# A two-layer backbone on one core: the last part of a layer split into latent and context tokens, each half's norm put beside products of the other half

## The chip, the cores and the metric

One core of one Trainium2 chip. The time is the device time of one execution in microseconds, median of the runs. TensorE (PE in the profile) does the matrix products, with its weight loads shown apart (PEld); VectorE is DVE, ScalarE is ACT, GpSimd is POOL, and SyncE (SP) issues most of the transfers.

## What is computed

Two layers over a stream of 256 context and 512 latent tokens of 1024 channels. The reference, cut:

```python
for l in range(DEPTH):                       # 2 layers
    ctx_out = l < DEPTH - 1                  # the last layer gives only latent tokens
    mod_l = split(silu(c) @ w_mod[l] + b_mod[l], 6); mod_c = split(silu(c_ctx) @ w_mod[l] + b_mod[l], 6)
    hc = modulate(xc, norm_mix_pre[l], mod_c[0], mod_c[1])
    hl = modulate(xl, norm_mix_pre[l], mod_l[0], mod_l[1])
    oc, ol = token_mixer(hc, hl, ..., w_in[l], rw, cv, at, w_branch[l], w_out[l], ctx_out)
    xl = xl + mod_l[2] * rms_norm(ol, norm_mix_post[l])
    hl = modulate(xl, norm_mlp_pre[l], mod_l[3], mod_l[4])
    xl = xl + mod_l[5] * rms_norm(sq_relu_mlp(hl, w_ff1[l], w_ff2[l]), norm_mlp_post[l])
    if ctx_out:                              # the same three lines for xc, with mod_c
        ...
return xl
def modulate(x, g, shift, scale): return rms_norm(x, g) * (1 + scale) + shift
# token_mixer: z = h @ w_in; three branches (RWKV-7, convolution, attention), each @ w_branch,
# summed with sigmoid gates (columns of z), then @ w_out
```

## The kernel before

All activations lie transposed: 128 channels on the partitions, eight such tiles k, tokens along the free axis, context in columns 0 to 255 and latent tokens in 256 to 767. `TOK` is 768. Layer 0 works on all 768 tokens, which a product takes as two pieces of 384; layer 1's last part works on the 512 latent ones (`T` = 512).

A float32 product is made of three products of a narrower format: activation and weight are split in a high and a low part (hh and hl or fh and fl, oh and ol; wh and wl), and high by high, low by high and high by low are summed. A tile of 128 output channels is 8 k x 3 products per piece. A weight tile comes as two halves of 256 KB (`weight_half`): a transfer into raw on SP's queue (two buffers), wh on ScalarE and wl on VectorE (three buffers). `gemm` makes a tile at once; `job` puts a tile in a list, and `fill(n)` takes n of its k steps from it, so that tiles can be woven between other work. The order in which each engine gets its instructions is settled by a scheduler when the program is built, which starts from the order of the code.

The last part of a layer goes: three branch projections (`branch` in `merge_phase`, with gates gt, sum in acc), acc halved and split into oh and ol, eight w_out tiles, the norm of their result (`ss_slow` sums squares, `rstd` makes 1/root as a column and TensorE spreads it into R), `post_norm` (scale acc, add to the residual X, square it again), a second `rstd`, `norm_h` (modulated and split into hh and hl). Then in `mlp_phase` four quarters q, each of eight ff1 tiles (squared relu, split into fh and fl) and eight ff2 tiles added into acc; and after the last quarter the same chain of norms again, now with the next layer's first modulation. Its hh and hl feed the next layer's projection, `rwkv_phase`. In that, tiles of z go to memory through `spill`; rows 28 to 31 of the list are four gate tiles, and `todo` and `SCHED` say how many tiles are made at which of eight head pairs.

The modulation vectors come from w_mod in steps of 1 MB (`mod_steps`, tile wmod, two buffers, loaded by ScalarE's queue): eight a group, 16 of them for layer 0 between the branch and w_out tiles, 24 for layer 1, one behind each ff1 tile of the first three quarters.

Of the kernel before, what the change touches and what calls it, by code (L numbers as in the profile page):

```python
# [8 lines left out]
F32 = mybir.dt.float32  # L9
# [9 lines left out]
D = 1024  # L19
# [29 lines left out]
         dict(open=1.2, first=0.4, mid=0.4, end=0.4, solve=34, early=5, tap0=0.8, tap1=0.8, merge=1.4, sums=0, grams=0, rest=9, ln=9, pad=1, last=0.85, tap2=1.1)]  # L49
# [27 lines left out]
class Kern:  # L77
# [48 lines left out]
    def dv(s, ap, T):  # L126

        return ap.rearrange("p (a b) -> p a b", b=384) if T == TOK else ap[:, CTX:TOK]

# [203 lines left out]

    def norm_h(s, sp, X, R, T, gs, sh, hh, hl):

        nc = s.nc
        o = TOK - T
        for k in range(KT):
            t = sp.tile([128, TOK], F32, tag="nt", name="nt", bufs=2)
            for b, t0, t1 in s.pieces(T, CTX):  # L340
                v = 1 if t0 < CTX else 0
                sl = slice(t0, t1)
                nc.vector.scalar_tensor_tensor(out=t[:, sl], in0=X[:, k, sl], scalar=gs[:, k, v:v + 1], in1=R[:, b, :t1 - t0], op0=ALU.mult, op1=ALU.mult)
                if k % 2:
                    nc.scalar.activation(out=t[:, sl], in_=t[:, sl], func=AF.Identity, bias=sh[:, k, v:v + 1])
                else:
                    nc.scalar.activation(out=hh[:, k, sl], in_=t[:, sl], func=AF.Identity, bias=sh[:, k, v:v + 1])  # L347
                    nc.vector.scalar_tensor_tensor(out=hl[:, k, sl], in0=t[:, sl], scalar=sh[:, k, v:v + 1], in1=hh[:, k, sl].bitcast(F32), op0=ALU.add, op1=ALU.subtract)
            if k % 2:
                s.split(hh[:, k, o:], hl[:, k, o:], t[:, o:], True)  # L350

    def post_norm(s, sp, A, X, R, T, gm, each):

        nc = s.nc
        o = TOK - T
        for k in range(KT):
            for b, t0, t1 in s.pieces(T, CTX):
                v = 1 if t0 < CTX else 0
                nc.vector.scalar_tensor_tensor(out=A[:, k, t0:t1], in0=A[:, k, t0:t1], scalar=gm[:, k, v:v + 1], in1=R[:, b, :t1 - t0], op0=ALU.mult, op1=ALU.mult)
            eng = nc.gpsimd if k % 2 else nc.vector  # L360
            eng.tensor_tensor(out=X[:, k, o:], in0=X[:, k, o:], in1=A[:, k, o:], op=ALU.add)
            each(k)
# [29 lines left out]
    def job(s, src, mh, ml, T, done, pre=None):  # L392

        s.halves += [(src, h) for h in range(2)]
        s.jobs += [(k, mh, ml, T, done, pre) for k in range(KT)]

    def fill(s, n=1):
        nc = s.nc
        for _ in range(min(n, len(s.jobs))):
            k, mh, ml, T, done, pre = s.jobs.pop(0)  # L400
# [8 lines left out]
            for w, m, f in ((wh, mh, 0), (wh, ml, 1), (wl, mh, 2)):  # L409
                a = m(k)  # L410
                for b, t0, t1 in s.pieces(T):
                    s.last_mm = nc.tensor.matmul(s.jps[:, b, :t1 - t0], lhsT=w[:, k % 4, :], rhs=a[:, t0:t1], start=k == 0 and f == 0, stop=k == KT - 1 and f == 2)  # L412
# [662 lines left out]
    def spill(s, l, r, T):  # L1075

        c0, t, f = s.spills[r]
        T = TOK if t else T
        s.in_job(l, c0, T, lambda ps: s.spill_done(r, T, f, ps))

    def spill_done(s, r, T, tanh, ps):
        nc = s.nc
        ft = s.stage()
        if tanh:
            nc.scalar.activation(out=s.dv(ft, T), in_=s.pv(ps, T), func=AF.Tanh, scale=0.5)
        else:
            nc.scalar.activation(out=s.dv(ft, T), in_=s.pv(ps, T), func=AF.Copy)
        nc.scalar.dma_start(s.z[128 * r:128 * r + 128, TOK - T:], ft[:, TOK - T:])


    def run(s):
# [13 lines left out]
        s.z = s.dp.tile([128 * len(s.spills), TOK], F32, name="z")  # L1105
        s.kp = lambda d: d.rearrange("(k p) t -> p k t", p=128)
# [15 lines left out]
        for l in range(DEPTH):  # L1122
# [5 lines left out]
            s.h_open()  # L1128
            s.mlp_phase(l, PP, T, acc, actx)
# [9 lines left out]
    def rwkv_phase(s, l, P, T):  # L1139
# [3 lines left out]
        with ExitStack() as rc:  # L1143
# [21 lines left out]
            todo = list(range(20)) + list(range(28, 36)) + list(range(20, 28))  # L1165

# [82 lines left out]
    def merge_phase(s, l, PP, T, acc):  # L1249
# [4 lines left out]
        with ExitStack() as mc:  # L1254
# [67 lines left out]
            drive(ln, 3)  # L1322
            s.fill(len(s.jobs))
            branch(1, *operand(lambda k: cvx[k]))
            for j in range(KT):
                s.fill(8)
                if steps:
                    steps.pop(0)()
            for k in range(KT):
                nc.vector.tensor_scalar(out=acc[:, k, o:], in0=acc[:, k, o:], scalar1=0.5, scalar2=None, op0=ALU.mult)  # L1330
            hs, ls = operand(lambda k: acc[:, k])
            s.ss = s.ps2()

            def done(j, ps):
                nc.scalar.activation(out=s.dv(acc[:, j], T), in_=s.pv(ps, T), func=AF.Copy)
                s.ss_slow(lp, s.ss, acc[:, j], j, T)
            for j in range(KT):
                s.job(i['w_out'][l, :, 128 * j:128 * j + 128], lambda k: hs[k], lambda k: ls[k], T, lambda ps, j=j: done(j, ps))
            for j in range(KT):
                s.fill(8)  # L1340
                if steps:
                    steps.pop(0)()
            if l == 0:
                s.mod_post(P)
            s.R = s.rstd(lp, s.ss, T, 1.0 / D, 0, CTX)

    def mlp_phase(s, l, PP, T, acc, actx):
# [5 lines left out]
        if not last:  # L1353
            PP.append(s.load_params(l + 1))
        X = actx.enter_context(tc.tile_pool(name="x", bufs=1)).tile([128, KT, TOK], F32, name="X")
        for k in range(KT):
            nc.sync.dma_start(X[:, k, o:], s.xT_d[128 * k:128 * k + 128, o:])
        with tc.tile_pool(name="n1", bufs=1) as sp:
            ss = s.ps2()
            s.post_norm(sp, acc, X, s.R, T, P['gm'][0], lambda k: s.ss_add(sp, ss, X[:, k], k, T))  # L1360
            R = s.rstd(sp, ss, T, 1.0 / D, 0, CTX)
            s.norm_h(sp, X, R, T, P['gs'][1], P['sh'][1], s.hh, s.hl)
        with tc.tile_pool(name="mlp", bufs=1) as sp:
            steps = [f for g in range(3) for f in s.mod_steps(l + 1, PP[l + 1], sp, g, 2)] if not last else []
            for q in range(4):
                fhs, fls = [], []
                for j in range(KT):
                    c = q * D + 128 * j
                    ps = s.gemm(i['w_ff1'][l, :, c:c + 128], lambda k: s.hh[:, k], lambda k: s.hl[:, k], T)
                    f = sp.tile([128, TOK], F32, tag="f", name="f", bufs=2)  # L1370
                    nc.scalar.activation(out=s.dv(f, T), in_=s.pv(ps, T), func=AF.Relu)
                    nc.vector.tensor_tensor(out=f[:, o:], in0=f[:, o:], in1=f[:, o:], op=ALU.mult)
                    fh = sp.tile([128, TOK], F32R, tag="fh", name="fh", bufs=8)
                    fl = sp.tile([128, TOK], F32R, tag="fl", name="fl", bufs=8)
                    s.split(fh[:, o:], fl[:, o:], f[:, o:])
                    fhs.append(fh)
                    fls.append(fl)
                    if steps:
                        steps.pop(0)()
                if q == 3:  # L1380
                    ss = s.ps2()
                for j in range(KT):
                    ps = s.gemm(i['w_ff2'][l, q * D:(q + 1) * D, 128 * j:128 * j + 128], lambda k: fhs[k], lambda k: fls[k], T)
                    if q == 0:
                        nc.scalar.activation(out=s.dv(acc[:, j], T), in_=s.pv(ps, T), func=AF.Copy)
                    else:
                        nc.vector.tensor_tensor(out=s.dv(acc[:, j], T), in0=s.dv(acc[:, j], T), in1=s.pv(ps, T), op=ALU.add)
                    if q == 3:
                        s.ss_slow(sp, ss, acc[:, j], j, T)
            if not last:  # L1390
                s.mod_pre(PP[l + 1])
                s.mod_post(PP[l + 1])
            s.R = s.rstd(sp, ss, T, 1.0 / D, 0, CTX, tag="sq")
        with tc.tile_pool(name="n2", bufs=1) as sp:
            if last:
                s.post_norm(sp, acc, X, s.R, T, P['gm'][1], lambda k: None)
                s.store_x(sp, X)
            else:
                ss = s.ps2()
                s.post_norm(sp, acc, X, s.R, T, P['gm'][1], lambda k: s.ss_add(sp, ss, X[:, k], k, T))  # L1400
                R = s.rstd(sp, ss, T, 1.0 / D, 0, CTX)
                N = PP[l + 1]
                s.norm_h(sp, X, R, T, N['gs'][0], N['sh'][0], s.hh, s.hl)
                nc.sync.dma_start(s.kp(s.xT_d), X)
        actx.close()
# [13 lines left out]
    def store_x(s, sp, X):  # L1419
        nc = s.nc  # L1420
        for t in range(4):
# [37 lines left out]
```

## Time and profile before

| | |
|---|---|
| median of 3 runs | 4373.27 us (4359.16 to 4374.07) |
| the profiled execution | 4372.14 us, span of its instructions 4370.4 us |
| mean granted TensorE clock | 0.963 |
| TensorE busy | 4141.8 us, 95% |
| VectorE, ScalarE, GpSimd busy | 2723.4 us, 1834.4 us, 287.1 us |

Busy time is an average over stages; the table says only that TensorE is nearly full. Times in the rows are from the start of the span. An idle time is put down to what ended last before the engine went on.

### The profile page before, as it was taken

To read this page: it belongs to the slowest core of one execution; us is meant where nothing else is said; L and a number is where in the kernel's file an instruction comes from. 1 tells how busy PE (TensorE), PEld (TensorE's weight loads), DVE (VectorE), ACT (ScalarE), POOL (GpSimd) and SP (SyncE) were. 2 spreads that over 40 slices of the span, in tenths; PEclk is the share of its full clock that TensorE was granted. 3 is DMA by queue.
4 is the path that set the end of the run, shared out by engine and by line. 5 is a ranking of instruction groups with operands and counts; after the bars stand their busy time and mean duration, and the time that the engine had idled before them with its cause. 6 is when DMAs were issued, how large, how long until landed. Compare 5 with 4: busy or idle time off the path is not lost.

```text
span 4370.4 us, 77114 instructions
## 1 busy us (share of the span) xinstructions
PE 4141.8 (95%) x31232; PEld 3410.5 (78%) x31232; DVE 2723.4 (62%) x5238; ACT 1834.4 (42%) x3586; POOL 287.1 (7%) x349
## 2 busy tenths in 40 slices
PE   6999999999998989899999899999999989898998
PEld 4888888888886679689999677887777765575886
DVE  3788888888855554332323577888888855554344
ACT  3444445444534442332223445555545534433332
POOL 0000000000001022200000100000000000121001
PEclk9999999999999999899999889999999979998998
DMA  4212211112134234343322221112221232242332
GB/s 165 78 47 63 64 53 60 51 55 63 59 100 163 69 120 160 110 152 126 102 86 63 72 70 51 58 59 60 66 62 57 73 119 74 65 140 61 97 94 80
DMA packets 443595, 367.73 MB, mean 84 GB/s; under 512 B 19662, under 2 KB 391528, under 8 KB 437096
## 3 DMA queue, kind: packets, MB, share of 16 engines
q1 hardware_dynamic: 422504, 283.10, 21.6%
q10 hardware_dynamic: 20736, 79.70, 5.0%
q8 instruction: 247, 4.05, 0.4%
q14 instruction: 108, 0.88, 0.1%
HBM read 301.38 MB, written 53.48 MB: 81 GB/s over the span
## 4 chain that ended last, share of the span: by engine, by line
PE 80%; DVE 9%; ACT 5%; issue 2%; DMA 2%; POOL 2%; SPq 0%; ACTq 0%; DVEq 0%; POOLq 0%
PE mm L412 31%; PE mm L389 20%; PE g L815 3%; PE g L633 2%; PE g L939 2%; PE sp L960 2%; PE g L928 2%; PE S L612 2%; PE sp L964 1%; PE yp L978 1%; PE yp L976 1%; PE g L850 1%; PE g L1044 1%; PE g L824 1%; PE g L234 1%
## 5 line engine op out<-in xcount | busy, mean ns | idle before, releaser
L328 ACT ACTIVATE wh<-raw 128x512 fp32r<-128x512 f32 x700 | 441.4, 631 | 1249.8 <-PE mm L389 565.5
L332 DVE TENSOR_TENSOR wl<-raw,wh 128x512 fp32r<-128x512 f32 x700 | 502.0, 718 | 697.6 <-ACT wh L328 685.3
L412 PE MATMUL mm<-hh,wh 128*128 128x384 f32 (+1 forms) x2072 | 647.5, 371 | 15.3 <-ACT hh L328 4.8
L412 PE MATMUL mm<-hl,wh 128*128 128x384 f32 (+1 forms) x2072 | 637.9, 367 | 6.1 <-POOL hl L330 6.1
L412 PE MATMUL mm<-hh,wl 128*128 128x384 f32 (+1 forms) x2072 | 634.8, 365 | 0.0
L471 DVE SCALAR_TENSOR_TENSOR cv<-u,dw,cv 128x783 f32<-128x783 f32 (+1 forms) x480 | 426.7, 889 | 2.8
L412 PEld LDWEIGHTS mm<-hh,wh 128*128 128x128 f32 x2072 | 377.6, 192 | 55.1 <-ACT hh L328 7.3
L412 PEld LDWEIGHTS mm<-hl,wh 128*128 128x128 f32 x2072 | 382.6, 192 | 38.0 <-POOL hl L330 8.8
L412 PEld LDWEIGHTS mm<-hh,wl 128*128 128x128 f32 x2072 | 383.0, 192 | 30.5 <-issue 3.2
L412 PE MATMUL mm<-oh,wh 128*128 128x384 f32 (+1 forms) x768 | 252.9, 384 | 9.5 <-DVE acc L1285 6.0
L412 PE MATMUL mm<-ol,wh 128*128 128x384 f32 (+1 forms) x768 | 239.9, 365 | 10.2 <-POOL ol L330 10.2
L389 PE MATMUL mm<-hh,wh 128*128 128x384 f32 (+1 forms) x768 | 239.5, 367 | 5.3 <-ACT hh L347 3.6
L389 PE MATMUL mm<-hl,wh 128*128 128x384 f32 (+1 forms) x768 | 238.3, 365 | 5.1 <-POOL hl L330 4.6
L412 PE MATMUL mm<-oh,wl 128*128 128x384 f32 (+1 forms) x768 | 238.8, 364 | 0.0
L389 PE MATMUL mm<-hh,wl 128*128 128x384 f32 (+1 forms) x768 | 235.8, 362 | 0.0
L389 PE MATMUL mm<-fh,wh 128*128 128x384 f32 (+1 forms) x768 | 229.9, 353 | 0.0
L389 PE MATMUL mm<-fh,wl 128*128 128x384 f32 (+1 forms) x768 | 229.9, 353 | 0.0
L389 PE MATMUL mm<-fl,wh 128*128 128x384 f32 (+1 forms) x768 | 229.5, 352 | 0.0
L815 PEld LDWEIGHTS g<-KR,BK 64*128 64x128 f32 x1536 | 157.3, 204 | 43.0 <-issue 33.7
L815 PE MATMUL g<-KR,BK 64*128 64x128 f32 (+1 forms) x1536 | 178.3, 306 | 5.2 <-DVE KR L808 3.1
L412 PEld LDWEIGHTS mm<-oh,wh 128*128 128x128 f32 x768 | 139.6, 189 | 51.2 <-ACT wh L328 13.6
L966 ACT ACTIVATE S<-sp,lam 128x64 f32<-128x64 f32 x352 | 92.9, 310 | 206.3 <-PE sp L964 199.4
(297 smaller groups left out, 7239.0 us busy)
## 6 DMA issues: line engine op xcount, KB each, us to landing
raw<-in_w_in_dram SPq DMA_DIRECT2D x316, 256.0 KB
raw<-in_w_ff_dram SPq DMA_DIRECT2D x256, 256.0 KB
wmod<-in_w_mod_dram ACTq DMA_DIRECT2D x48, 1024.0 KB
raw<-in_w_branch_dram SPq DMA_DIRECT2D x96, 256.0 KB
z<-f ACTq DMA_DIRECT2D x40, 384.0 KB
gt<-z SPq DMA_DIRECT2D x24, 384.0 KB
raw<-in_w_out_dram SPq DMA_DIRECT2D x32, 256.0 KB
z<-f ACTq DMA_DIRECT2D x32, 256.0 KB
```

The lines of the kernel that those rows point to most:

```text
L328: s.last_hi = nc.scalar.activation(out=hi, in_=src, func=AF.Copy)
L332: nc.vector.tensor_tensor(out=lo, in0=src, in1=hi.bitcast(F32), op=ALU.subtract)
L389: nc.tensor.matmul(ps[:, b, :t1 - t0], lhsT=w[:, k % 4, :], rhs=a[:, t0:t1], start=k == 0 and f == 0, stop=k == KT - 1 and f == 2)
L412: s.last_mm = nc.tensor.matmul(s.jps[:, b, :t1 - t0], lhsT=w[:, k % 4, :], rhs=a[:, t0:t1], start=k == 0 and f == 0, stop=k == KT - 1 and ...
L471: s.tap_pin(nc.vector.scalar_tensor_tensor(out=hold['c'], in0=u[:, k:k + L], scalar=w(k), in1=hold['c'], op0=ALU.mult, op1=ALU.add))
L612: nc.tensor.matmul(sps[:, b, :384], lhsT=lq, rhs=kT[kv][:, 384 * b:384 * b + 384], start=True, stop=True)
L633: nc.tensor.matmul(op[:, :nq], lhsT=V[:, kk, kv * 128:kv * 128 + 128], rhs=PT[:, kk, :nq], start=kk == 0, stop=kk == nk // 128 - 1)
L815: nc.tensor.matmul(gp[h][:, q, 0:n, :], lhsT=BK[ROWS[h], 4 * g + q].rearrange("p a b -> p (a b)"), rhs=KR[ROWS[h], 0:n, 4 * g + q, :], sta ...
L928: nc.tensor.matmul(wu[ROWS[h], q - q0], lhsT=TT[ROWS[h], q, :], rhs=KM[ROWS[h], q].rearrange("p a b -> p (a b)"), start=True, stop=True)
L939: nc.tensor.matmul(ap[ROWS[h], q - q0, 0:n, :], lhsT=W[ROWS[h], q, :], rhs=GB[ROWS[h], h, q, 0:n, :], start=True, stop=True)
L960: nc.tensor.matmul(sp[ROWS[h], d], lhsT=GB[d][:, h, q[d], 0, :], rhs=UV[d][:, h * 12 + q[d], :], start=d == 0, stop=d == 1 and k == 0)
L966: nc.scalar.activation(out=Sn[:, d], in_=sp[:, d], func=AF.Copy, scale=Q['lam', d][:, q[d]:q[d] + 1])
```

## The change

`mlp_phase` is gone. `tail_phase` now does all from the halving of acc to the end of the layer, with all its tiles as jobs, and pieces of tokens given as lists: latent (256 to 767), context (0 to 255) or full.

- In layer 0 the eight w_out tiles are done for latent tokens first, then for context tokens; the latent half's two norms (`residual`, a generator, woven in by `weave`) are written beside the context products. Then four ff1 tiles for latent tokens, with the context half's norms beside, and the same four for context tokens; the other tiles are whole. The weights of tiles done in two halves are loaded and split twice.
- The last ff2 quarter of layer 0 is done in the same way. Beside the context half's last norm stand gate tiles 28 to 31 of layer 1 for latent tokens, which leave layer 1's own list; `rest` in `SCHED[1]` goes from 9 to 12.
- Layer 1's last part has latent tokens alone and goes through the same code, with nothing beside its norms.
- The residual's add is VectorE's for all k; before, every second was GpSimd's.
- The 16 modulation steps of layer 0 are done among the branch tiles, up to two a tile, and none in w_out. Those of layer 1 are written behind the ff1 tiles of quarters 1 to 3; before, 0 to 2.
- The row sums, R and the one-column products use another tile of PSUM (S and g in the rows).

```diff
-         dict(open=1.2, ..., rest=9, ln=9, pad=1, last=0.85, tap2=1.1)]
+         dict(open=1.2, ..., rest=12, ln=9, pad=1, last=0.85, tap2=1.1)]
...
+    def residual(s, sp, A, X, ss, pcs, gm, nxt=None):
+
+        nc = s.nc
+        R = s.rstd_p(sp, ss, pcs)
+        yield 2.0
+        s2 = s.g([128, 512]) if nxt else None
+        for k in range(KT):
+            for t0, t1, r in R:
                 v = 1 if t0 < CTX else 0
+                nc.vector.scalar_tensor_tensor(out=A[:, k, t0:t1], in0=A[:, k, t0:t1], scalar=gm[:, k, v:v + 1], in1=r, op0=ALU.mult, op1=ALU.mult)
+            for t0, t1 in s.spans(pcs):
+                nc.vector.tensor_tensor(out=X[:, k, t0:t1], in0=X[:, k, t0:t1], in1=A[:, k, t0:t1], op=ALU.add)
+            if nxt:
+                sq, n = s.squares(sp, X[:, k], pcs)
+                nc.tensor.matmul(s2[0:1, :n], lhsT=s.ones, rhs=sq, start=k == 0, stop=k == KT - 1)
+            yield 0.5
+        if nxt:
+            R = s.rstd_p(sp, s2, pcs)
+            yield 2.0
+            for k in range(KT):
+                s.norm_k(sp, X, R, k, nxt[0], nxt[1], s.hh, s.hl)
+                yield 0.5
...
+            if lat:
+
+                todo = [r for r in todo if r not in s.early]
...
+            for k in range(KT):
+                nc.vector.tensor_scalar(out=acc[:, k, o:], in0=acc[:, k, o:], scalar1=0.5, scalar2=None, op0=ALU.mult)
+                s.split(ops[k][0][:, o:], ops[k][1][:, o:], acc[:, k, o:], k % 2 == 1)
...
+            out_jobs(lat, h[0])
+            flush()
+            if T == TOK:
+                out_jobs(ctx, h[1])
+            s.weave(0.6, s.residual(sp, acc, X, h[0]['ss'], lat, P['gm'][0], nxt(P, 1)))
+            flush()
+            if T == TOK:
+                some = range(4)
+                ff1_jobs(0, lat, f0, some)
+                s.weave(0.6, s.residual(sp, acc, X, h[1]['ss'], ctx, P['gm'][0], nxt(P, 1)))
+                flush()
+                ff1_jobs(0, ctx, f0, some)
+            ff1_jobs(0, full, f0, range(len(some), KT))
+            ff2_jobs(0, full, f0)
+            flush()
...
+            ff2_jobs(3, lat, fs, h[0])
+            flush()
+            if not last:
+                ff2_jobs(3, ctx, fs, h[1])
+            s.weave(0.6, s.residual(sp, acc, X, h[0]['ss'], lat, P['gm'][1], n))
+            flush()
             if last:
+                s.store_x(sp, X, range(4))
             else:
+                for r in s.early:
+                    s.spill(l + 1, r, lat)
+                s.weave(0.6, s.residual(sp, acc, X, h[1]['ss'], ctx, P['gm'][1], n))
                 nc.sync.dma_start(s.kp(s.xT_d), X)
+                flush()
```

What the scheduler makes of it, at three places. The first is ScalarE's queue at the start of w_out in layer 0; oh and fh are the high parts of the halved acc, wh of a weight, modsb a row of the modulation. Before:

```order
L328 ACTIVATE wh<-raw 128x512 x2
L232 DMA wmod<-in_w_mod_dram 128x2048
L328 ACTIVATE oh<-acc 128x768 x6
L328 ACTIVATE wh<-raw 128x512 x2
L239 ACTIVATE modsb<-g 128x512
L232 DMA wmod<-in_w_mod_dram 128x2048
L328 ACTIVATE oh<-acc 128x768
L328 ACTIVATE wh<-raw 128x512 x2
L1335 ACTIVATE acc<-mm 128x768
```

And with the change:

```order
L344 ACTIVATE wh<-raw 128x512 x2
L248 DMA wmod<-in_w_mod_dram 128x2048
L344 ACTIVATE wh<-raw 128x512 x4
L255 ACTIVATE modsb<-g 128x512
L344 ACTIVATE fh<-acc 128x768 x8
L344 ACTIVATE wh<-raw 128x512
L248 DMA wmod<-in_w_mod_dram 128x2048
L1445 ACTIVATE acc<-mm 128x512
L344 ACTIVATE wh<-raw 128x512
```

Before, one of the eight splits stands further ahead (not shown), six before modsb among the weights of the last branch tile, one behind it; now all eight stand behind modsb in one block, ahead of the next weight.

The second place is TensorE in layer 0 at the first norm's row sums (S or g from sq and ones, 512 columns). Before there are no products between them and the first ff1 tile:

```order
L311 MATMUL S<-sq,ones 1x512
L291 MATMUL g<-ones,row 128x1 x6
L298 MATMUL mm<-cst,rs 128x128 x6
L389 MATMUL mm<-hh,wh 128x384 x2
L389 MATMUL mm<-hl,wh 128x384 x2
```

With the change the latent norm's row sums stand among context products of w_out:

```order
L428 MATMUL g<-sq,ones 1x512
L486 MATMUL mm<-fl,wh 128x256
L486 MATMUL mm<-fh,wl 128x256
L428 MATMUL g<-sq,ones 1x512
L486 MATMUL mm<-fh,wh 128x256
L486 MATMUL mm<-fl,wh 128x256
L486 MATMUL mm<-fh,wl 128x256
L486 MATMUL mm<-fh,wh 128x256
L486 MATMUL mm<-fl,wh 128x256
L428 MATMUL g<-sq,ones 1x512 x6
```

Two row sums stand alone; six stand together, and no product is between them.

The third place is TensorE in layer 0 behind the first norm, where products meet layer 1's modulation steps (wmod; four rows' products are one step). Before, a step stands between ff1 products:

```order
L234 MATMUL g<-wmod,sc_17840 32x512 x4
L389 MATMUL mm<-hh,wh 128x384 x2
L389 MATMUL mm<-hl,wh 128x384 x2
L389 MATMUL mm<-hh,wl 128x384 x2
L389 MATMUL mm<-hh,wh 128x384 x2
L389 MATMUL mm<-hl,wh 128x384 x2
```

With the change, in the context half's norm, between latent ff1 products (R by L386, 128x128):

```order
L486 MATMUL mm<-hl,wh 128x512
L486 MATMUL mm<-hh,wl 128x512
L192 MATMUL g<-cst,ra 128x128
L193 MATMUL g<-cst,rb 128x77
L250 MATMUL g<-wmod,sc_19177 32x512
L386 MATMUL S<-cst,rs 128x128 x2
L250 MATMUL g<-wmod,sc_19177 32x512 x23
L486 MATMUL mm<-hh,wh 128x512
L486 MATMUL mm<-hl,wh 128x512
```

And the loads of these steps in ScalarE's queue, behind the second root (row) of that norm:

```order
L376 ACTIVATE row<-g 1x256
L344 ACTIVATE wh<-raw 128x512 x2
L248 DMA wmod<-in_w_mod_dram 128x2048
L368 ACTIVATE hh<-nt,mod 128x256
L365 ACTIVATE nt<-nt,mod 128x256
L248 DMA wmod<-in_w_mod_dram 128x2048
L344 ACTIVATE hh<-nt 128x256
L368 ACTIVATE hh<-nt,mod 128x256
L248 DMA wmod<-in_w_mod_dram 128x2048
L365 ACTIVATE nt<-nt,mod 128x256
```

24 products, six steps, stand together now around the context half's R, and each load of wmod stands between operations of that norm on ScalarE.

## Rows read from the trace of the kernel before

**Rows 1.** The page's first line, and the chain that ended last, by engine.

```profile
span 4370.4 us, 77114 instructions
...
PE 80%; DVE 9%; ACT 5%; issue 2%; DMA 2%; POOL 2%; SPq 0%; ACTq 0%; DVEq 0%; POOLq 0%
```

**Rows 2.** Busy time by stretch, with granted clock (PEclk), DMA share and rate.

```profile
core 0: us, PE busy (x) PEld busy (x) DVE busy (x) ACT busy (x) POOL busy (x), PEclk, DMA share, GB/s
1730.00:1894.00 164.00, 145.44 (x754) 115.46 (x750) 63.42 (x116) 54.08 (x81) 33.27 (x22) 0.91 0.41 137
1809.00:1866.00 57.00, 39.96 (x140) 22.99 (x139) 36.10 (x82) 23.92 (x37) 14.49 (x8) 0.73 0.18 65
1866.00:2426.00 560.00, 557.49 (x3230) 529.17 (x3228) 170.70 (x222) 143.19 (x210) 13.22 (x13) 1.00 0.33 105
2355.00:2498.00 143.00, 122.73 (x609) 104.30 (x608) 64.18 (x113) 52.51 (x77) 25.87 (x22) 0.90 0.20 64
2480.00:3520.00 1040.00, 1010.29 (x9751) 808.59 (x9749) 845.04 (x1771) 535.43 (x1143) 32.82 (x100) 0.96 0.21 63
```

**Rows 3.** The same view for the products' tile mm; last, for tile wmod.

```profile
1840.00:1858.00 18.00, 12.23 (x35) 9.60 (x36) 7.76 (x14) 0.00 (x0) 0.53 0.00 1
1940.00:1970.00 30.00, 30.00 (x175) 30.00 (x174) 0.00 (x0) 3.18 (x4) 1.00 0.23 66
4000.00:4290.00 290.00, 290.00 (x1258) 236.25 (x1258) 11.00 (x16) 20.90 (x36) 1.00 0.33 95
...
1730.00:1894.00 164.00, 11.80 (x92) 1.73 (x88) 0.91 0.41 137
```

**Rows 4.** VectorE's and ScalarE's groups: count, busy us, mean ns.

```profile
L328 ACT ACTIVATE oh<-acc 128x768 fp32r<-128x768 f32 x8 | 6.7, 847 | 11.2 <-DVE mc L263 5.3 <-PE mm L412 3.1 <-DVE acc L1330 2.8
...
L347 ACT ACTIVATE hh<-nt,mod 128x512 fp32r<-128x512 f32 x8 | 5.7, 711 | 0.3
...
L328 ACT ACTIVATE wh<-raw 128x512 fp32r<-128x512 f32 x179 | 113.0, 631 | 508.5 <-PE mm L389 374.6 <-PE mm L412 114.8 <-DMA raw<-in_w_branch_dram 13.3
...
L359 DVE SCALAR_TENSOR_TENSOR acc<-acc,mc,mm 128x512 f32<-128x512 f32 x16 | 11.8, 738 | 0.0
...
L359 DVE SCALAR_TENSOR_TENSOR acc<-acc,mc,mm 128x256 f32<-128x256 f32 x16 | 7.6, 473 | 3.4 <-PE mm L298 3.4
...
L361 DVE TENSOR_TENSOR X<-X,acc 128x512 f32<-128x512 f32 x8 | 5.5, 690 | 0.0
...
L819 DVE TENSOR_TENSOR GL<-g,masks 128x256 f32<-128x256 f32 x96 | 40.4, 421 | 51.3 <-PE g L815 50.8
```

**Rows 5.** Timeline of layer 1's first norm: start, duration, what, idle before.

```profile
3947.03 0.40 PE L412 MATMUL mm<-oh,wl 128*128 128x512 f32 x1
...
3949.12 1.02 PE L311 MATMUL S<-sq,ones 128*1 128x512 f32 x2 [1.69 <-ACT sq L320]
...
3956.28 1.41 DVE L359 SCALAR_TENSOR_TENSOR acc<-acc,mc,mm 128x512 f32<-128x512 f32 x2 [1.21 <-PE mm L298]
...
3968.87 0.59 ACT L287 ACTIVATE row<-S 1x512 f32<-1x512 f32 x1 [1.11 <-PE S L311]
...
3974.26 1.41 DVE L343 SCALAR_TENSOR_TENSOR nt<-X,mc,mm 128x512 f32<-128x512 f32 x2 [1.21 <-PE mm L298]
```

**Rows 6.** Timeline of the opening: modulation loads and TensorE's steps.

```profile
54.76 2.05 ACTq L232 DMA_DIRECT2D wmod<-in_w_mod_dram  x3
...
59.54 1.07 PE L234 MATMUL g<-wmod,sc 128*32 128x512 f32 x8 [0.47 <-DMA wmod<-in_w_mod_dram]
...
62.03 1.07 PE L234 MATMUL g<-wmod,sc 128*32 128x512 f32 x8 [1.42 <-DMA wmod<-in_w_mod_dram]
```

**Rows 7.** TensorE's waits in layer 1's head stage: us in total, times, longest.

```profile
PE g L901 <- DVE Z L868: 5.0, 5, 1.2
```

**Rows 8.** Timeline of layer 1's last residual, VectorE and GpSimd.

```profile
4349.33 1.41 DVE L359 SCALAR_TENSOR_TENSOR acc<-acc,mc,mm 128x512 f32<-128x512 f32 x2 [1.21 <-PE mm L298]
...
4356.57 1.65 POOL L361 TENSOR_TENSOR X<-X,acc 128x512 f32<-128x512 f32 x1 [0.27 <-DVE acc L359]
```

More of the change, by code (lines that the diff above doesn't have):

```diff
@@ L48 @@
 SCHED = [dict(open=1.3, first=0.55, mid=0.5, end=0.4, solve=26, early=4, tap0=1, tap1=1, merge=1.2, sums=0, grams=0, rest=9, ln=9, pad=1, last=1.15, tap2=1),
-         dict(open=1.2, first=0.4, mid=0.4, end=0.4, solve=34, early=5, tap0=0.8, tap1=0.8, merge=1.4, sums=0, grams=0, rest=9, ln=9, pad=1, last=0.85, tap2=1.1)]
+         dict(open=1.2, first=0.4, mid=0.4, end=0.4, solve=34, early=5, tap0=0.8, tap1=0.8, merge=1.4, sums=0, grams=0, rest=12, ln=9, pad=1, last=0.85, tap2=1.1)]
 def shape_constants():
@@ new lines, in squares, with ss_tile @@
+    def squares(s, sp, x, pcs):
+        sq, o = sp.tile([128, TOK], F32, tag="sq", name="sq", bufs=2), 0
+        for t0, t1 in s.spans(pcs):
+            s.nc.scalar.activation(out=sq[:, o:o + t1 - t0], in_=x[:, t0:t1], func=AF.Square)
+            o += t1 - t0
+        return sq[:, :o], o
+    def ss_tile(s, sp, hold, x, k, pcs):
+        sq, n = s.squares(sp, x, pcs)
+        if k == 0:
+            hold['sa'] = sp.tile([128, 512], F32, tag="sa", name="sa", bufs=1)[:, :n]
+            s.nc.gpsimd.tensor_copy(hold['sa'], sq)
+        elif k < KT - 1:
+            s.nc.gpsimd.tensor_tensor(out=hold['sa'], in0=hold['sa'], in1=sq, op=ALU.add)
+        if k >= KT - 2:
+            if k == KT - 2:
+                hold['ss'] = s.g([128, 512])
+            s.nc.tensor.matmul(hold['ss'][0:1, :n], lhsT=s.ones, rhs=hold['sa'] if k == KT - 2 else sq, start=k == KT - 2, stop=k == KT - 1)
@@ L394, in job @@
         s.halves += [(src, h) for h in range(2)]
-        s.jobs += [(k, mh, ml, T, done, pre) for k in range(KT)]
+        s.jobs += [(k, mh, ml, T if isinstance(T, list) else s.pieces(T), done, pre) for k in range(KT)]
     def fill(s, n=1):
@@ L1321, in merge_phase @@
             branch(2, *operand(load(s.oat)))
-            drive(ln, 3)
-            s.fill(len(s.jobs))
+            for _ in range(4):
+                for _ in ln:
+                    s.fill(3)
+                    break
+            while s.jobs:
+                for _ in range(2):
+                    next(ln, None)
+                s.fill(8)
+                if steps:
+                    steps.pop(0)()
+            for _ in ln:
+                pass
             branch(1, *operand(lambda k: cvx[k]))
@@ L1326, in merge_phase, with tail_phase @@
                 s.fill(8)
[L1327 to L1342, printed above, removed]
+                for _ in range(2 if len(steps) > KT - j else 1):
+                    if steps:
+                        steps.pop(0)()
             if l == 0:
                 s.mod_post(P)
-            s.R = s.rstd(lp, s.ss, T, 1.0 / D, 0, CTX)
-    def mlp_phase(s, l, PP, T, acc, actx):
+    def tail_phase(s, l, PP, T, acc):
         nc, tc, i, P = s.nc, s.tc, s.i, PP[l]
@@ L1352, in mlp_phase @@
         s.lo_pool = False
[L1353 to L1362, printed above, removed]
```

191 lines of the change are left out of this document (121 added, 70 removed).

## Prediction

> **What bounds the kernel now.** I read the chain that ended last first [rows 1]: 80% of the span is TensorE, 9% VectorE, 5% ScalarE. So the kernel ends when its products end, and what can be won lies in the few places where TensorE stands still. The busy times by stretch say where [rows 2]. The MLP of layer 0 is full: 557.5 of 560 us at clock 1.00. Just ahead of it, from 1809 to 1866, TensorE is busy for 40.0 of 57 us, at a mean clock of 0.73: this is the first norm, in which the residual is added and all 768 tokens are normalised while nothing else is ready. The second norm, after the MLP, has the same look within 2355 to 2498. Layer 1 has the same two places, but with 512 tokens and nothing to put there.
>
> To measure such a place I take the stretch from the first product before a norm to a point where products run steadily again, and take off what the products themselves need. The pitch comes from full stretches [rows 3]: 30.00 us for 174 products of 384 columns is 0.172 us each, 290.00 us for 1258 of 512 columns 0.2305 us. For 256 columns there is no row; a straight line through the two gives 0.1135 us, and it can be neither below half of 512's nor above 384's. By that line one piece of 512 and one of 256 cost what two of 384 cost (0.344 us), so splitting the products costs TensorE nothing in itself.
>
> - Interval 1, 1730 to 1894: eight w_out tiles and four ff1 tiles, 12 x 48 = 576 products or 99.1 us, and 11.8 us of modulation steps [rows 2, 3]. 164.0 - 99.1 - 11.8 leaves a loss of 53.1 us.
> - Interval 2, 2355 to 2498: eight tiles of the last ff2 quarter and three of layer 1's projection, 528 products or 90.8 us of 143.0; loss 52.2 us.
>
> If both norms vanished, 105 us or 2.4% would be won. The question is how much of that two half norms, each with products of the other half beside it, give back.
>
> **The change part by part.**
>
> *Start of w_out in layer 0.* Before, seven of acc's eight tiles were split while branch products ran. Now all eight splits stand in one block on ScalarE behind the last modulation step (first place of the order). Each is 0.847 us [rows 4], and a tile of 512-column products needs 3 x 0.2305 = 0.69 us per k, so for eight k the products follow ScalarE: 8 x 0.16 = 1.3 us, plus the chain from the last branch product through transposes, halving, split and low part, about 4 us by estimate, from five operations of 0.7 to 0.85 us. With the weight split among them I take 7 us. The loads of X now stand in SP's queue among the w_out weights; for that I add 2 us (0 if they land beside, 4 if a weight waits for them). The 16 modulation steps are only moved into the branch products: 11.8 us there, 11.8 us less in interval 1.
>
> *First half norm, latent tokens, beside 192 context products.* One norm's chain without any cover is to be read in layer 1 [rows 5]. From the end of the last product (3947.03 + 0.40) to the start of the residual at 3956.28 are 8.8 us: evacuation, square, row sum, reciprocal root, its transposes. The residual is now VectorE's alone: 8 x (0.738 + 0.690) = 11.4 us [rows 4]. From the last row sum's copy at 3968.87 to the norm at 3974.26 are 5.4 us, to which the last square and sum add 1.7 and two weight splits on VectorE 1.3: 28.6 us so far. The norm itself then is ScalarE's: four even k at 0.711 and four odd at the same and a copy of 512 columns, 0.631 as a weight's, are 8.2 us, about five weight splits of 0.631 and the context tiles' copies and squares add some 7, the first and last VectorE or GpSimd operation 2: 17 us. Together **46 us**. The products that can lie beside it are 192 x 0.1135 = 21.8 us, so TensorE still stands idle for half of it. Where, the order shows (second place): six row sums stand one behind another, and TensorE can't pass them until VectorE has added six more tiles.
>
> *Second half norm, context, beside four latent ff1 tiles.* Reciprocal root 8.8, residual 8 x (0.473 + 0.421) = 7.2 [rows 4], sums and second root about 4: 20 us to the second R. In this stretch the order holds 48 latent products, 11.1 us. And then comes what the diff doesn't tell: six of the first eight modulation steps of layer 1 have moved here in one block, behind one another (third place), with two wmod buffers. Before they came one per ff1 tile. What a block costs, the opening shows [rows 6]: issued at 54.76, steps at 59.54, 62.03 and so on, 4.8 us from issue to the first and 2.5 us to the next. With two buffers a step waits for the one two earlier and a load: 1.07 + 4.8 = 5.9 us for each two, so six end after 2 x 5.9 + 2.5 + 1.07 = 15.4 us, of which 6.4 us are their own work (1.07 each), paid earlier instead of later. The block also holds ScalarE, in whose queue the loads stand between the norm's operations; so VectorE and the context norm are behind it. After it 48 latent products (11.1) and the 96 context ones (10.9): **57.4 us**.
>
> Interval 1 then is 7 + 2 + 192 x 0.2305 (44.3) + 46 + 57.4 = 156.7 us, less 6.4 for the steps that leave the MLP: 150.3 us, against 164.0 - 11.8 = 152.2. **Gain 2 us**, with bounds: without a stall in the block +9, with a shorter latent half norm (weight splits in gaps) +5, with 512-column waits for X -2, with the 256-column products at 0.172 us -5 (only those behind the second norm are on the path).
>
> *Weights loaded twice.* 40 more half tiles cost 40 x 0.631 on ScalarE and as much on VectorE. Inside the norms they are counted above. In the plain latent products they are hidden: a half lasts 12 x 0.2305 = 2.8 us there.
>
> *End of layer 0.* 44.3 us of latent ff2, 46 us of half norm beside context ff2, and then the context norm: 20 us and some 7.5 for its ScalarE part, 27.5, over four gate tiles of 24 x 0.2305 = 5.5 us each, 22.1 together, which fit. Then 144 projection products, 24.8 us. Sum 142.6 against 143.0: **0 us**. But the 22.1 us of gate products no longer stand in layer 1. What is saved there is bounded by 0 and 22.1. The stage from 2480 to 3520 has TensorE busy for 1010 of 1040 us [rows 2], which speaks for nearly all; that TensorE waited for VectorE's solve before the merge product for 5.0 us in all [rows 7] says that in some head pairs products are only cover, and there fewer of them save nothing. I take **13 us**.
>
> *Layer 1's tail.* No context there, so no cover. Before, VectorE and GpSimd shared the last residual from 4349.33 to 4358.22 [rows 5, 8], 8.9 us; now VectorE alone needs 11.4: 2.5 us more. In the first norm the row sums were last anyway, 0.5 us. The splits at the start as above, at 512 columns: 1. **Loss 4 us** (2 to 6).
>
> Sum: 2 + 0 + 13 - 4 = 11 us faster. The profiled execution took 4372.1 us (4370.4 of span), 1.1 us under the median of the runs. So I forecast **4362 us**, 0.3% less.
>
> **A rule against the row.** In the first norm's stretch products were sparse, and from 1840 to 1858 the granted clock was 0.53, its 35 products busy for 12.2 us, 0.35 each or twice the pitch [rows 3]: the 1.2 GHz level, after TensorE had done little but row sums and transposes. The Trainium skill, "TensorE: Matmul & The Clock Gate", section "HAM oscillation — how this bites in real kernels", says that gaps between bursts of products bring the gate back to half rate and that the next burst starts there. The trace agrees with it here. It speaks against a change that spreads products thinly through a norm: by the rule the sum would be that of the first rival below, by the slack in the row it stays the forecast.
>
> **The rivals.**
>
> *Slower: the thin products run at 1.2 GHz.* In the latent half norm of either interval 192 context products would take 2 x 21.8 = 43.6 us, and row sums, root products and transposes stand between them, about 13 us (eight sums at 1.02 [rows 5], the rest the two roots): 57 us instead of 46, +11 each. In the context norms 48 latent products behind the block and half of the gates at half rate add 11 each. Together +44, so 4406 us. For it: clock 0.73 now. Against: while a half norm is at its VectorE chain TensorE has slack, and half rate costs nothing until the products take longer than the chain; it decides only if the granted clock stays near 0.5 for more than half of a half norm.
>
> *Faster: the norms hide better.* Modulation loads land beside the norm and the block stalls nothing (+9), the gate tiles save all of their 22 us (+9), and ScalarE's evacuations and weight splits find gaps in both latent half norms (+5 each): 28 us on top, 4334 us. For it: the DMA queues are busy for a fifth to two fifths of the time, and layer 1's head stage is nearly full.
>
> *The gates save nothing.* Layer 1's head stage is paced by VectorE (solve, merge) and the four missing tiles turn into waits: 4375 us, no change. For it, [rows 7]; against, the 1010 of 1040 us.
>
> **Chances.** Forecast 0.39, faster rival 0.30, gates save nothing 0.13, slow clock 0.18. A difference of 0.5%, 22 us, is about what a measurement of this kernel can tell from no change; 4351 to 4395 is inside it. Of the forecast's share 0.09 lies below, nothing much above; of the slow rival's nearly all above, and 0.03 of the gates'. So faster 0.38, within 0.5% 0.41, slower 0.21. Its own range is 4345 to 4378; the range over the cases 4328 to 4404.
>
> **What would show it.** In the profile after: the stretch of the first half norm near 46 us with TensorE about half busy, and a wait of TensorE for VectorE or ScalarE at the six row sums; a wait for "DMA wmod" at several steps in the context norm, some 9 us in sum; a first w_out product 7 us behind the last branch product; layer 1's head stage some 13 us shorter, with more waiting for the solve; the end after the last product 2 to 3 us longer. I am wrong if a half norm takes much less than 46 us (it overlaps further than the chain of layer 1 allows), if the granted clock is 0.5 through the half norms, or if layer 1's head stage is not shorter.

## The result and the profile after

The changed kernel took 4398.45 us (median of 4 runs, 4395.95 to 4406.05) against 4372.16 us of before: ratio 1.0069, interval 1.0046 to 1.0093. It is slower by 26 us; I had forecast 11 us faster.

The profiled execution took 4395.95 us, its span 4394.2 us. Most of the chain of work isn't followed back in this page, so I read the two traces by stretches, cut at the same products in both (first product of a stage to first of the next, in us):

| stretch | before | after | difference |
|---|---|---|---|
| start to the first branch product of layer 0 | 1360.0 | 1351.9 | -8.0 |
| to the first w_out product (with 16 modulation steps of 1.07 now here, 8 before) | 370.0 | 382.9 | +12.9 |
| to the fifth ff1 tile: first norm | 165.1 | 165.0 | -0.1 |
| to the last ff2 quarter | 460.0 | 456.9 | -3.1 |
| to the 96th whole-width (384 columns) projection product of layer 1: second norm | 132.9 | 153.1 | +20.2 |
| layer 1's head stage, to its first branch product | 1118.8 | 1124.7 | +5.9 |
| to layer 1's first ff1 product | 369.1 | 369.0 | -0.1 |
| to the last ff2 product | 365.2 | 360.8 | -4.4 |
| to the end | 29.3 | 29.9 | +0.6 |

The differences add up to 23.9 us, the two spans differ by 23.8. The first row isn't put down to the change: in the fourteen kernels of the experiments, with either code, it came out between 1349 and 1362. Three lines of the table, steps moved included, concern the first norm: together +9.7. The second norm and layer 1's head stage concern the gate tiles: +26.1. By these two traces this is the whole loss.

The busy times by stretch of the changed kernel answer to [rows 2], with its columns; the second line is the latent half of the first norm, the third ten us within it, the last but one the latent half of the second norm, the last the gate tiles:

```profile
1735.00:1900.00 165.00, 145.16 (x705) 101.58 (x706) 88.88 (x177) 75.47 (x144) 31.07 (x26) 0.91 0.44 143
1785.00:1834.00 49.00, 41.56 (x237) 30.04 (x235) 34.09 (x67) 27.74 (x53) 10.25 (x11) 0.90 0.28 81
1823.00:1833.00 10.00, 7.42 (x30) 5.68 (x29) 6.62 (x9) 5.65 (x11) 3.92 (x4) 0.50 0.31 90
2357.00:2510.00 153.00, 133.80 (x659) 103.36 (x659) 79.13 (x173) 65.02 (x115) 22.34 (x30) 0.97 0.34 105
2403.00:2451.00 48.00, 38.59 (x239) 27.98 (x238) 35.38 (x76) 26.02 (x46) 10.51 (x11) 1.00 0.28 82
2451.00:2489.00 38.00, 31.67 (x128) 21.00 (x127) 21.65 (x62) 16.48 (x36) 3.48 (x12) 0.91 0.50 164
```

A half norm with its 192 context products takes 48 to 49 us (forecast 46), at a mean granted clock of 0.90 and 1.00; in the first, ten us near its end ran at the 1.2 GHz level. TensorE is busy for four fifths of a half norm, not for half. And the stretch with the 96 gate products, 22.1 us by the pitch, takes 38.

The chain of the latent half is to be seen in the timeline of the changed kernel. It answers to [rows 5]: last latent product 1784.95, residual from 1793.69, the six row sums in a line up to 1805.9, norm from 1813.35, last low part done at 1830.67. The last two lines are the end of the context products:

```profile
1784.95 0.39 PE L486 MATMUL mm<-fh,wl 128*128 128x512 f32 x1
...
1793.69 1.41 DVE L423 SCALAR_TENSOR_TENSOR acc<-acc,mc,S 128x512 f32<-128x512 f32 x2
...
1796.22 1.40 DVE L423 SCALAR_TENSOR_TENSOR acc<-acc,mc,S 128x512 f32<-128x512 f32 x2
...
1799.57 3.82 PE L428 MATMUL g<-sq,ones 128*1 128x512 f32 x8
...
1804.04 1.88 PE L428 MATMUL g<-sq,ones 128*1 128x512 f32 x4 [0.64 <-ACT sq L397]
...
1813.35 1.41 DVE L363 SCALAR_TENSOR_TENSOR nt<-X,mc,S 128x512 f32<-128x512 f32 x2 [0.81 <-PE S L386]
...
1829.40 1.27 POOL L346 TENSOR_TENSOR hl<-nt,hh 128x512 fp32r<-128x512 f32 x1
...
1834.00 0.28 PE L486 MATMUL mm<-fl,wh 128*128 128x256 f32 x1
1834.12 0.28 PE L486 MATMUL mm<-fh,wl 128*128 128x256 f32 x1
```

Two tiles of the residual take 2.53 us (1793.69 to 1796.22), not 2 x 1.43: in the trace, VectorE's operations overlap a little. The chain itself ended 45.3 us after the latent products (1785.34 to 1830.67), as forecast; the context products ended another 3.7 us later, at 1834.40. So it was TensorE that ended the stretch.

### The profile page after: what moved, and what is told of

The parts are those of the page before. It is cut to its first block, busy times and chain, and to the rows that moved or that the text cites. A ratio compares the mean times of both kernels' runs of the same rounds, so it can differ in the third digit from the quotient of the medians.

```text
span 4394.2 us, 77534 instructions
## 1 busy us (share of the span) xinstructions
PE 4153.1 (95%) x31232; PEld 3397.3 (77%) x31232; DVE 2764.7 (63%) x5382; ACT 1869.2 (43%) x3686; POOL 258.6 (6%) x355
## 5 line engine op out<-in xcount | busy, mean ns | idle before, releaser
L486 PE MATMUL mm<-hh,wh 128*128 128x384 f32 (+2 forms) x2840 | 890.1, 369 | 20.9 <-ACT wh L344 9.9
L486 PE MATMUL mm<-hl,wh 128*128 128x384 f32 (+2 forms) x2840 | 879.6, 365 | 3.3 <-POOL hl L346 3.3
L486 PE MATMUL mm<-hh,wl 128*128 128x384 f32 (+2 forms) x2840 | 881.9, 366 | 0.8 <-DVE wl L348 0.7
L486 PEld LDWEIGHTS mm<-hh,wh 128*128 128x128 f32 x2840 | 521.5, 192 | 89.1 <-ACT wh L344 23.8
L486 PE MATMUL mm<-fh,wl 128*128 128x512 f32 (+2 forms) x960 | 312.7, 358 | 9.5 <-DVE wl L348 9.5
L486 PE MATMUL mm<-fh,wh 128*128 128x512 f32 (+2 forms) x960 | 311.2, 357 | 6.7 <-ACT fh L344 3.9
L486 PE MATMUL mm<-fl,wh 128*128 128x512 f32 (+2 forms) x960 | 312.0, 357 | 1.7 <-POOL fl L346 1.4
L486 PEld LDWEIGHTS mm<-fh,wl 128*128 128x128 f32 x960 | 179.7, 190 | 32.5 <-DVE wl L348 12.8
L486 PEld LDWEIGHTS mm<-fh,wh 128*128 128x128 f32 x960 | 179.3, 190 | 31.8 <-ACT wh L344 6.1
L486 PEld LDWEIGHTS mm<-fl,wh 128*128 128x128 f32 x960 | 179.9, 190 | 25.3 <-issue 3.5
L941 DVE TENSOR_TENSOR A<-A,Z 128x30 f32<-128x30 f32 (+14 forms) x480 | 158.8, 331 | 12.5
```

The source lines that it names most:

```text
L941: nc.vector.tensor_tensor(out=X[:, k + 1:, 0:k], in0=X[:, k + 1:, 0:k], in1=tm, op=ALU.add)
```

## The experiments

Medians and ratios are set against before, measured alongside; stretches are those of the table. "Second norm" and "head stage" are its fifth and sixth rows.

**The gate tiles.** Five runs part the two ends of the move, the rate `rest`, and the tiles' worth. Of layer 1's tiles the first seven head pairs get 32 less `rest`: 23 with rest 9, 20 with rest 12; what remains is left for the end of the stage.

```diff
# gates back, rest 9                         # rest 9 alone: only the last line
-        s.early = list(range(28, 32))
+        s.early = []
-  rest=12
+  rest=9
```

> The change without its gate tiles at the end of layer 0: all 36 tiles in layer 1's head stage, rest back to 9; the split norms stay. Cover theory (in layer 1's head the four tiles cost nothing because they lie beside VectorE's work and keep TensorE at its clock; at the end of layer 0 they cost what they don't hide): head stage back near the 1119 us of before (1124.5 with the change), the end of layer 0 shorter by 22 us less the 5 to 15 us that the tiles hid there, total 4375 to 4388. Rate theory (rest 12 made the head stage slow, the moved tiles do save their time): head stage 1119 or more, and total no better than 4385 to 4395.

4375.85 us, ratio 1.0001 (0.9990 to 1.0013): the whole loss is gone. Second norm 134.3 us instead of 153.1: the 22.1 us of gate products had hidden 3.3. Head stage 1113.7.

> The change with rest left at 9 instead of 12, so that layer 1's tiles go to the head pairs at the old rate; gate tiles still at the end of layer 0. Rate theory: the head stage falls from 1124 to about 1105 us (before's 1119 less 13), total about 4380. Cover theory: the head stage stays within 1116 to 1128, total 4390 to 4402.

4383.08 us, ratio 1.0026 (1.0013 to 1.0039), head stage 1108.0, second norm 153.6. Both theories lose a part: `rest` 12 cost the head stage 16.7 us, as the rate theory said, but against the 1113.7 with all tiles there the four tiles are worth only 5.7, not 13 or 22.

```diff
# gates twice, with rest 9
-                todo = [r for r in todo if r not in s.early]
+                pass
```

> The four gate tiles computed twice: at the end of layer 0 as in the change, and again in layer 1's head stage, rest 9; 96 products of 512 columns (22 us) more than the change. Cover theory: they are free in the head stage, which takes before's 1119 us or less than the change's 1124, total 4388 to 4400, not above the change. Rate theory: 13 us above the run with rest 9 alone, total about 4393 against 4380. If TensorE alone bounds the head stage: 4420.

4391.73 us, ratio 1.0046 (1.0029 to 1.0064), head stage 1112.3, 4.3 more than without these tiles there: for 22.1 us of products. Above the run with rest 9, as the rate theory said, but by 9 us, of which the trace has 4 in the head stage.

```diff
# before, four tiles left out; rest 12 or 9
+                todo = [r for r in todo if not 28 <= r < 32]
+        if T == SEQ and 32 <= r < 36:
+            nc.scalar.dma_start(s.z[128 * r - 512:128 * r - 384, TOK - T:], ft[:, TOK - T:])
```

> The kernel before with the four gate tiles (rows 28 to 31) of layer 1 left out and rest 12; rows 32 to 35 are stored in their place, so these gates are not the reference's. It prices what the four tiles cost in layer 1's head stage with nothing else moved. My prediction says 13 us less than before, 4359; TensorE alone as the bound 22 us less, 4350. Cover theory: nothing is saved, 4368 to 4378.

> The kernel before with the four gate tiles left out of layer 1 (rows 32 to 35 stored in their place, so these gates are not the reference's) and rest 9. With rest 12 it was 4373.6, head stage 1117. If rest 12 itself slows the head pairs (by 15 us, as between the change and its run with rest 9): head stage about 1105, total about 4362. If rest 12 cost the change 15 us only by the order that came out of it: head stage 1112 to 1117, total 4369 to 4375.

With rest 12: 4373.56 us, ratio 0.9997 (0.9983 to 1.0011), head stage 1117.2. With rest 9: 4366.85 us, 0.9989 (0.9978 to 0.9999), head stage 1108.9, 9.9 under before's 1118.8 (in a trace of the fastest of its ten executions; by the ratio the run is 5 us faster). So the tiles are worth 4 to 10 us of head stage where `rest` stays, and nearly nothing where it goes to 12 with them.

**Why rest 12 costs.** Two runs: before with rest 12 and nothing else, and the change with three other tiles made a second time, so that the pairs are as full as with rest 9.

```diff
# three tiles twice, in the change, with rest=9
                 todo = [r for r in todo if r not in s.early]
+                todo = todo[:8] + [5, 6, 7] + todo[8:]
```

> The kernel before with rest 12 and nothing else changed. Cover theory: the head stage rises from 1118.8 by what rest 12 cost in the two pairs of runs so far, 8 to 17 us, total 4381 to 4390. If rest 12 matters only with four tiles fewer: within 3 us of before, 4370 to 4376.

> The change with three query tiles of layer 1 (rows 5 to 7) computed a second time in the head stage, so that the seven pairs get 23 tiles as with rest 9, and the last pair 7 as with rest 12: 72 products of 512 columns, 16.6 us of TensorE, more than the change. Cover theory (what the head pairs lack with rest 12 is products that keep TensorE busy and its granted clock at 2.4 GHz): head stage shorter than the change's 1124.7 in spite of the work, about 1108 to 1116, total 4383 to 4391. If TensorE's work decides: head stage 1141, total 4415. If it is the seven tiles left for the last pair that cost: head stage 1125 or more.

Before with rest 12: 4381.40 us, ratio 1.0026 (1.0015 to 1.0036), head stage 1127.2, 8.4 longer; against this run the four tiles left out with rest 12 (1117.2) are worth 10.0 us too. The change with three tiles twice: 4384.80 us, ratio 1.0035 (1.0019 to 1.0052); head stage 1113.6. 72 products or 16.6 us more work, and 11 us less time than with the change. One place where the time goes is to be seen in one head pair of layer 1, from its sixth merge product (g from Z and GL) to its seventh, in four kernels: busy time by stretch with the columns of [rows 2], first for all instructions, then for the products' tile mm alone. Before:

```profile
3257.20:3380.20 123.00, 120.96 (x1238) 96.12 (x1238) 104.53 (x223) 65.57 (x143) 4.80 (x12) 1.00 0.21 63
...
3257.20:3380.20 123.00, 66.09 (x264) 46.91 (x264) 0.69 (x1) 7.32 (x11) 1.00 0.21 63
```

Before with rest 12:

```profile
3254.00:3382.80 128.80, 123.56 (x1227) 98.34 (x1227) 104.31 (x223) 65.74 (x143) 5.32 (x12) 0.95 0.20 59
...
3254.00:3382.80 128.80, 65.48 (x253) 46.63 (x253) 0.68 (x1) 6.71 (x10) 0.95 0.20 59
```

The change:

```profile
3282.70:3411.70 129.00, 123.55 (x1228) 98.63 (x1228) 104.35 (x224) 65.86 (x143) 5.33 (x12) 0.95 0.20 59
...
3282.70:3411.70 129.00, 65.79 (x253) 46.72 (x253) 0.68 (x1) 6.72 (x10) 0.95 0.20 59
```

The change with three tiles twice:

```profile
3264.10:3386.60 122.50, 120.59 (x1237) 95.79 (x1237) 104.33 (x224) 65.65 (x143) 4.33 (x12) 1.00 0.21 63
...
3264.10:3386.60 122.50, 65.84 (x263) 46.29 (x263) 0.69 (x1) 7.33 (x11) 1.00 0.21 63
```

With 263 or 264 products the pair takes 123 us at clock 1.00, with 253 it takes 129 at 0.95, in these four traces. VectorE does the same in all four (104.3 to 104.5 us). Ten products less are 2.3 us less work, but TensorE's other operations take 58.1 instead of 54.9 us (123.56 - 65.48 against 120.96 - 66.09), and its idle time rises from 2.0 to 5.2. How much of that is the lower clock and how much another order isn't parted: the scheduler's order differs too. Nor is it a rule. In before with the tiles left out and rest 12, which has the change's order in the head pairs, the same 253 products took 125.2 us:

```profile
3264.00:3389.20 125.20, 120.24 (x1227) 95.99 (x1227) 104.28 (x223) 65.84 (x143) 5.32 (x12) 0.97 0.23 68
```

And with the tiles left out and rest 9, 264 products took 127.4 us at 0.96. That rest 12 costs time is shown by the totals; that it does so by the granted clock isn't.

**The modulation block.** Each step is tied behind the product ahead of it:

```diff
+                if l and q == 0:
+                    s.behind(g, s.last_mm)
```

> The change with each modulation step of layer 1 tied behind the product ahead of it on TensorE, so that no step comes before the second MLP quarter, one behind each ff1 tile. Block theory: the 9.1 us of waiting for wmod in the context norm go, and 6.4 us of steps move from there into the MLP; first w_out product to fifth ff1 tile falls from 165.0 to about 150 us, the rest of the MLP rises from 456.9 to 463, total 9 us less than the change (4398 to 4389). Chain theory: the context norm is as long without the block, TensorE then waits for hh and hl instead; the interval falls by the 6.4 us alone, to about 158, and the total by 0 to 3 us.

> No gate tiles at the end of layer 0, rest 9, and modulation steps spaced: the split norms with nothing else that costs. Block theory: 9 us less than the run with the gates back, 4375.9, so about 4367, 8 us under before. Chain theory: 4373 to 4377, no better than before.

With the gates as in the change: 4392.96 us, ratio 1.0048 (1.0033 to 1.0064). First norm 165.0 to 155.8, MLP 456.9 to 463.2: the steps' own 6.4 us moved, and only 2.9 were won. With the gates back: 4371.43 us, ratio 1.0003 (0.9994 to 1.0013). So the block theory failed in what it promised: the wait was there and went, and another of the same length took its place. TensorE's longest wait in the first norm, in the change, and then with the steps spaced and the gates back (us in total, times, longest):

```profile
PE g L250 <- DMA wmod<-in_w_mod_dram: 9.1, 4, 5.2
```
```profile
PE mm L488 <- ACT f L1456: 9.1, 1, 9.1
```

f is the copy of a latent ff1 tile out of PSUM. It stood on ScalarE behind all but the last of the context norm's operations, and the third tile's products had to wait for its place.

> The change with rest 9, steps spaced, and the store of X behind the last norm of layer 0 issued from GpSimd's queue instead of SyncE's, so that the weights behind it don't queue after 3 MB. If the store holds back the last gate tile's weights: the wait of 6.3 us for wh among the gate tiles goes, and the interval from the last ff2 quarter to the fifth projection tile falls from 153 to about 147 us. If ScalarE's own queue (its norm operations stand ahead of wh) holds it: the wait stays, 151 to 154. Total 4368 to 4376; gates worth moving only if it is under the run without them.

4377.89 us, ratio 1.0011 (1.0002 to 1.0021). Second norm 152.4. The wait for wh fell from 6.3 to 1.0 us, so the store had held it back, but a wait for the convolution's taps, another load, of 6.3 us took its place.

**Fuller pairs.** 

> The split norms with spaced modulation steps and all gate tiles in layer 1, with rest 6: 26 tiles to the seven pairs, 5 left for the last. The run with rest 9 was 4371.4, head stage 1117.9. Cover theory carried further: fuller pairs, clock nearer 1.00, head stage 1108 to 1116, total 4362 to 4370, which would be under before. If the pairs are already full with rest 9: head stage 1118 to 1126, total 4371 to 4380.

4371.84 us, 1.0003 (0.9991 to 1.0014), head stage 1119.3: nothing more is won beyond rest 9, and the pair shown above, now with 290 products, takes 133.5 us at 0.95.

**The order of the evacuations.** `weave` lets n k-steps of products into the code for each unit of the norm. At 0.6 some 7 of 32 or 64 fell into a norm, and the rest, with their evacuations, behind it. All three runs have spaced steps and rest 9.

```diff
-  s.weave(0.6, s.residual(sp, acc, X, h[1]['ss'], ctx, P['gm'][0], nxt(P, 1)))
+  s.weave(2.6, ...)          # first run: this one. Second: both latent norms at 5.2 too.
                              # Third: also the gates again, their norm at 2.6.
```

> No gate tiles, spaced steps, rest 9, and in layer 0's context norm the weave rate at 2.6 instead of 0.6, so that the latent ff1 tiles' evacuations on ScalarE stand between the norm's operations and not behind all of them. Queue theory (the 9.1 us wait is ScalarE's order, not its amount of work): the wait goes, first w_out product to fifth ff1 tile falls from 155.5 to 147 to 150 us, total 4363 to 4368. Chain theory (ScalarE and VectorE have that much work in the norm): the wait only moves to hh and hl, 153 to 157 us, total 4369 to 4375.

> As the run before, and both latent norms of layer 0 woven at 5.2 instead of 0.6, so that the context tiles' copies and squares come earlier. Queue theory: another 2 to 5 us in each, total 4355 to 4364. Chain theory: the latent norm gets longer by the work put in between, total 4370 to 4380.

> As the run before with the gate tiles at the end of layer 0 again (rest 9), woven at 2.6. Queue theory: the gates hide most of their 22 us, the interval from the last ff2 quarter to the fifth projection tile falls from 153 to 138 to 145 us, total 4352 to 4362. Chain theory: 150 to 154 us, total 4374 to 4382.

First: 4362.74 us, ratio 0.9979 (0.9967 to 0.9991), first norm 155.5 to 147.3. Second: **4358.35 us, ratio 0.9968 (0.9957 to 0.9980)**, first norm 141.9, second 130.5; faster than both kernels. Its largest wait in the first norm is 3.1 us:

```profile
PE mm L488 <- DVE wl L350: 3.1, 3, 1.4
```

Third: 4367.09 us, ratio 0.9994 (0.9983 to 1.0004), second norm 144.4. The gates now hide 8.2 of 22.1 us (144.4 - 130.5 = 13.9 are paid). The queue theory holds for the norms; the gate tiles stay a loss.

**How far one trace goes.** Several runs have the same order of instructions on TensorE, VectorE and ScalarE from the first to the eighth of layer 1's merge products. Their head stages, in us (the other runs have orders of their own):

| order in the head pairs | runs, in the order of the text | head stage |
|---|---|---|
| all tiles, rest 9 | before, gates back, gates twice, gates back with steps spaced, weave first and second | 1118.8, 1113.7, 1112.3, 1117.9, 1119.4, 1121.4 |
| four tiles out, rest 9 | rest 9 alone, store moved, weave third | 1108.0, 1108.4, 1125.6 |
| four tiles out, rest 12 | the change, before less four, steps spaced | 1124.7, 1117.2, 1126.7 |

So one order gives stages up to 18 us apart, at a mean granted clock of 0.94 (1108.0) and 0.92 (1125.6); the last trace of the second line is of an execution of 4382.73 us, 16 above its run's median. A difference of 4 to 10 us between two head stages is therefore weak by itself; the medians carry the verdicts.

## Why the prediction was wrong

- **The gates save 13 us in layer 1: this step failed, and with it the sign.** It took a busy TensorE (1010 of 1040 us, [rows 2]) for a bound, and it put the rate that belongs to the move, `rest` from 9 to 12, at nothing without a reason. The medians, each above that of before measured alongside, part the loss: 0.9 us for the split norms and the tail with the gates in their old place (I had 2), 8.1 us with the gates moved and rest 9, 26.3 us with rest 12, which is the change. So moving the tiles cost some 7 us where I had 13 saved, and rest 12 some 15 to 18 us on top. In the head stage the tiles save 4 to 10 us with rest 9, as far as single traces tell, and nothing with rest 12 (5.9 more with the change, 1.6 less in before). I had not looked at what `rest` does to each pair; it alone costs 8 us of head stage in before and 17 in the change (10 and 15 by the medians). My third rival had the saving at nothing; for this step it was nearest, and my own sign of being wrong, a head stage that is not shorter, is there.
- **The gate tiles fit into the context norm: failed.** I counted that norm at 27.5 us whether or not tiles lie beside it. Without them TensorE reached the projection 20 us after the last context product (2459.8 to 2479.6 in the run with the gates back), with them 38: their weights and copies stand in the norm's queues, and the last tile waits 6.3 us for its weight behind the 3 MB store. Hidden 3.3 us, where I had 22. Nor were there 22 us to fill: in those 20 us without tiles TensorE is busy for 9.6 with the norm's own sums and spreads, which leaves some 10 us of idle time. In that run (columns of [rows 2]):

```profile
2459.80:2479.60 19.80, 9.59 (x33) 3.39 (x33) 12.25 (x46) 5.54 (x14) 0.00 (x0) 0.67 0.40 147
```

- **The half norms: sizes nearly right, TensorE's slack not.** Start stall and latent tiles 54.4 us against 53.3; latent half 49 and 48 us against 46. The chain of VectorE and ScalarE took 45.3 us in both, but TensorE, which I had idle for half of it, was busy for 41.6 of 49 and ended behind it. Context half to the second R 20 us, as forecast, but 65.6 us in all against 57.4: the block took 19 us where I had 15.4, and the 48 latent and 96 context products behind it 13.4 each where I had 11.1 and 10.9. So the first norm's three stretches lost 9.7 us where I had a gain of 2.
- **The modulation block: seen, priced at 9 us, its wait found at 9.1.** But it was no cost of its own: taking it away won 2.9. Behind it stood ScalarE's order, a wait that I had not named as next.
- **The slow clock: there, but small.** By the Trainium skill's rule (TensorE: Matmul & The Clock Gate, "HAM oscillation — how this bites in real kernels"), that the gate falls to half rate in gaps between bursts of products, I looked for it in the norms. The trace agrees in that the clock did fall to the lower level there: for ten us near the end of the first latent half, and behind the waits for wmod and for wh, after each of which some nine products started 0.427 us apart instead of 0.2305. That is some 2 us in each of the three places, not 44. The measured 4398 us lies near that rival's 4406, and inside the range over the cases only because of it; that is luck, the loss came from elsewhere.
- **Layer 1's tail: +4 forecast, -3.9 measured.** VectorE alone needs 1.27 us a tile, so the last residual took 10.2 us instead of 8.9 and the stretch to the end grew by 0.6 us, not 2.5. Why the MLP's start became faster by 4.4 I haven't tested.

## What to carry to other kernels

Products taken out of a stage in which they lie beside another engine's chain can save much less than their duration (here 4 to 10 of 22 us), and what is changed along with them, here a rate, can cost more: price both by runs that leave them out or change them alone. When a wait is to be removed, look for what stands behind it: in the first norm a wait for ScalarE's copies took the place of 9 us of waiting for modulation weights, in the second a wait for the taps that of 6 us for a weight. Only the order of the evacuations won the first one, 8 us. Work put beside a norm needs its copies between the norm's operations, not behind them; and before it is put there, count how long TensorE is idle, not how long the norm lasts.

## What was unexpected of the hardware

One order of instructions in the head pairs took 1108 us in one trace and 1126 in another, at a mean granted clock of 0.94 and 0.92. A head pair with ten products less took 6 us more, at a granted clock of 0.95 instead of 1.00, in the change and in before with rest 12, and 2 us more in a third trace; the kernel that does 72 products twice is faster than the one that does them once. The 256-column products ran at 0.12 us each (1834.00 to 1834.12 above), over the 0.1135 of my straight line; that line already fell below half of 512's pitch (0.115), the bound I had set it.
